# Two-input elementwise work moved from GpSimd to VectorE, and squares from GpSimd to ScalarE, in a hybrid DeltaNet trunk

## The chip, the cores and the metric

The kernel runs on one core of a Trainium2 chip. The metric is the device time of one execution in microseconds; the median of three runs is taken. The profile gives the span of one profiled execution, from its first to its last instruction.

## The reference

One layer works on 256 tokens of width 2048, in float32. The part that the change touches is the first RMS norm and the gated DeltaNet branch:

```python
h = rms_norm(x, norm_mix_g)             # x * rsqrt(mean(x * x)) * gain
z = h @ w_in                            # 2048 -> all branches' inputs
qkv = silu(causal_depthwise_conv(gdn_qkv, conv_w))
...
decay = exp(where(incl, g[:, None] - g[None, :], -inf))
L = where(strict, (k * beta) @ k.T * decay, 0)
sol = triangular_solve(L + eye, rhs, lower=True, unit_diagonal=True)
intra = (q @ k.T) * decay
# then a scan over chunks: v_new = u - w S;  o = q_dec S + intra v_new;  S = S exp(g) + k_dec v_new
```

Eight heads of dimension 128 go through this. Beside it stand a spatial gating branch and a stick-breaking attention branch; gates, output projections and a squared-ReLU MLP of width 8192 follow. Those are not touched.

## The kernel before

Every product with a weight matrix is streamed. A block of weights is loaded on SP's queue into `raw` (three buffers), ScalarE rounds a piece of it into `hi` (line 154), VectorE takes the rest into `lo` (the subtraction in `split_w`, recorded under line 65, the helper `tt`), and TensorE multiplies with both. `hi` and `lo` have six buffers each, and a piece is split four pieces ahead of its use (`LA = 4`). So ScalarE's `hi` waits until TensorE has given a buffer back, VectorE's `lo` waits for `hi`, and TensorE's next piece waits for `lo`.

Everything else, the DeltaNet among it, is background work: generators in the queue `side`, from which `pump` takes one step after each piece of a product. On TensorE the order is the order in which the code is written, the product pieces and the background steps interleaved. On the other engines the framework's scheduler writes the order of each engine's queue ahead of time; only in the first product are VectorE's and ScalarE's own instructions kept in the order of the code too. Each engine then runs its queue strictly in order on the chip.

In the first product x arrives in eight chunks of two 128-row tiles. For each, `split_scaled` writes the high part on ScalarE (line 239) and the low part on VectorE (line 241). After each second chunk `x_squares` squares four tiles and adds them into `sq`, on GpSimd except for the last square; the sum ends in `ssx`, which `row_norms` needs for the reciprocal row norms.

`gdn_half` does four heads, and runs twice. Its two-input work on GpSimd is: `gm` (triangle mask times gate, high and low part, for two chunks), `kb`, `rkm` and the scaling of the decay `dec` (named `e` in rows) for two chunks, `kde` and `kbg`, and the substitution. For the substitution the matrix `LT` goes by DMA through a DRAM scratch `scrL` into `lb`, so that the 64 diagonal blocks of 16 x 16 lie on partitions of their own; then come 15 steps of one product `pr` and one subtraction into `tb`, 30 instructions each of which needs the one before:

```python
for j in range(15):
    n, m = 15 - j, j + 1
    pv = pr[:, 0 : n * m].rearrange("p (i s) -> p i s", i=n)
    tt(pv, lb[:, j, m:16].unsqueeze(2)..., tb[:, j : j + 1, 0:m]..., ALU.mult, nc.gpsimd)
    tt(tb[:, m:16, 0:m], tb[:, m:16, 0:m], pv, ALU.subtract, nc.gpsimd)
    if j % 2:
        yield
```

`tb` and its transpose `ub` (a GpSimd copy) go back through `scrT` and `scrU` into `Tm` and `Um`, by DMAs on GpSimd's queue. TensorE's first product with `Tm` stands at a fixed place in TensorE's order, after a number of product pieces. `add_halves` and `conv_silu` share three buffers (`half`) that ScalarE fills and VectorE empties.

Of the kernel before, what the change touches and what calls it, by code (L numbers as in the profile page):

```python
# [15 lines left out]
P = 128  # L16
# [4 lines left out]
def tile_hybrid_trunk(  # L21
# [47 lines left out]

    # ------------------------------------------------ background work queue  # L70
    side = deque()
# [9 lines left out]
    def pump_until(n):  # L81
        """run until at most n pieces of background work are left"""
        while len(side) > n:
            pump(1)
# [7 lines left out]

    # ------------------------------------------------ constants
    ident = cp.tile([P, P], F32, name="ident")
# [5 lines left out]

    # the tensor engine is clocked up only under work: give it some while the first loads run
    ones = cp.tile([P, P], F32, name="ones")
# [15 lines left out]
    def split_T(dst, k0, nk, pt, scale=None):  # L118
        """dst[:, k0:k0+nk] = the exact high and low parts of the (scaled) psum tile pt [P, nk, 256]"""
        if scale is None:  # L120
            nc.scalar.copy(dst[:, k0 : k0 + nk, 0, :], pt)
            tt(dst[:, k0 : k0 + nk, 1, :], pt, dst[:, k0 : k0 + nk, 0, :].bitcast(F32), ALU.subtract)
        else:
            for i in range(nk):
                s = scale[:, k0 + i : k0 + i + 1]
                nc.scalar.activation(dst[:, k0 + i, 0, :], pt[:, i, :], AF.Copy, scale=s)
            for i in range(nk):
                s = scale[:, k0 + i : k0 + i + 1]
                nc.vector.scalar_tensor_tensor(
                    dst[:, k0 + i, 1, :], pt[:, i, :], s, dst[:, k0 + i, 0, :].bitcast(F32),  # L130
                    op0=ALU.mult, op1=ALU.subtract,
                )

    # ------------------------------------------------ streamed products
    # Weights are split into exact high and low parts LA pieces ahead of the products that use them.
    LA = 4
# [7 lines left out]
    def flush():  # L144
        while pipe:
            pipe.popleft()()
# [11 lines left out]
    def gemm(lhs, w, b, done, before=None, rate=0):  # L158
        """done([psum of token tile t]) gets act times block b of w, tokens on partitions"""
        ps = []  # L160
# [32 lines left out]
    def gemm_T(act, w, b, done, g0=0, ng=None, rate=0):  # L193
        """done([psum of 128 columns each]) gets (act times block b of w)^T, its low-part half on the right"""
        ps = []
# [38 lines left out]

    # ------------------------------------------------ x^T and its row norms
    def split_scaled(dst, src, scale, k0, nk):
        """dst[:, k] = the exact high and low parts of scale[:, k] src[:, k]"""
        for k in range(k0, k0 + nk):
# [16 lines left out]
    def x_chunk(c, stage):  # L255
# [4 lines left out]
        else:  # L260
            split_scaled(actT, xs, g1, 2 * c, 2)
            if c % 2:
                x_squares(c // 2)

    hl = lhs_of(actT)
# [11 lines left out]
    def row_norms():  # L277
        """1 / rms of x's rows, along the free axis (rb) and on partitions (r1); then they scale the first product"""
        yield from rest(10)
# [12 lines left out]
        yield  # L292

    def x_squares(c):
        s4 = xp.tile([P, 4, T], F32, tag="sqc", name="sqc", bufs=2) if c else sq
        xc = xs[:, 4 * c : 4 * c + 4]
        if c < 3:
            tt(s4, xc, xc, ALU.mult, nc.gpsimd)
        else:
            nc.scalar.activation(s4, xc, AF.Square)  # L300
        if c:
            tt(sq, sq, s4, ALU.add, nc.gpsimd)
        if c == 3:
            tt(sq[:, 0:2], sq[:, 0:2], sq[:, 2:4], ALU.add, nc.gpsimd)
            tt(ssx, sq[:, 0], sq[:, 1], ALU.add, nc.gpsimd)

# [7 lines left out]
    with tc.manual_schedule(engines={ET.PE, ET.DVE, ET.Activation}):  # L314
        gemm(hl, w_ag0, 0, first_done, before=x_chunk, rate=1)
    flush()
    xctx.close()
    nc.gpsimd.dma_start(ab_bc, a_dt.partition_broadcast(P).rearrange("p o h -> p (o h)"))

    # ------------------------------------------------ more constants  # L320
    tri_gt_full = cp.tile([P, P], F32, name="tri_gt_full")
# [17 lines left out]

    # ------------------------------------------------ branch inputs, transposed  # L340
    brctx = ExitStack()
    brp = brctx.enter_context(tc.tile_pool(name="brp", bufs=1))
    aT = brp.tile([P, 8, 2, T], F32R, name="aT")

    # ================================================ gated DeltaNet
    gt0ctx = ExitStack()
# [3 lines left out]

    # lvl[b][s, c] = 1 where s lies in the first and c in the second half of one 2b block, in 64 x 64 blocks
    lvl = {}
# [24 lines left out]

    # scratch for moving the 16 x 16 diagonal blocks of a 64 x 64 block onto partitions of their own and back
    NB = 64
# [26 lines left out]
    def gates_ab():  # L406
# [9 lines left out]
        nc.scalar.activation(nega, ab_bc[:, 0:8], AF.Exp)  # L416
        # log1p(e) = 2 artanh(e / (2 + e))
        d = gp.tile(sh, F32, name="sp_d")
# [31 lines left out]
    def conv_silu(zt, cb0, dst):  # L450
        """causal convolution along the free axis, and SiLU; zt [P, 4, T] is scaled by the row norms first"""
        for j in range(4):
# [17 lines left out]
    def gdn_half(hf, tiles):  # L470
        """heads 4 hf .. 4 hf + 3, in chunks of 128, as tiles come in"""
        hs = slice(4 * hf, 4 * hf + 4)
# [23 lines left out]

        # decay[s, c] = exp(g_c - g_s) for s <= c
        dec = []
        ck = conv_silu(tiles["k"], 8 + 4 * hf, kTt)
        for t in range(NT):  # L500
            gms = []
            for part in (gh.bitcast(F32), gl):
                gm = t2k("gm", F32R)
                tt(gm, col(tri_le), row(part[:, t, hs]), ALU.mult, nc.gpsimd)
                gms.append(gm)
# [29 lines left out]
        for t in range(NT):  # L535
            kb = t2k("kb")
            tt(kb, kraw[:, t], row(brk[:, t]), ALU.mult, nc.gpsimd)
            rkm = t2k("rkm")
            tt(rkm, col(tri_le), row(rk[:, t]), ALU.mult, nc.gpsimd)
            tt(dec[t], dec[t], rkm, ALU.mult, nc.gpsimd)  # L540
            kbs.append(kb)
            yield
# [24 lines left out]

        # T = (I + L)^-1 and U = T^T: 16 x 16 blocks by substitution, then doubled to 128
        lb = gp.tile([NB, 16, 16], F32, tag="lb", name="lb")
# [21 lines left out]
        for j in range(15):  # L591
# [5 lines left out]
                tb[:, j : j + 1, 0:m].broadcast_to([NB, n, m]),  # L597
                ALU.mult, nc.gpsimd,
            )
            tt(tb[:, m:16, 0:m], tb[:, m:16, 0:m], pv, ALU.subtract, nc.gpsimd)  # L600
            if j % 2:
# [14 lines left out]
        kde = gp.tile([P, 4, HD], F32, tag="kde", name="kde")  # L616
        tt(kde, kraw[:, 0], row(f2), ALU.mult, nc.gpsimd)
        tt(kbg, kraw[:, 1], row(f1), ALU.mult, nc.gpsimd)
        tiles["k free"] = True
# [25 lines left out]
        for b in (16, 32):  # L645
# [4 lines left out]
            yield from rest(2)  # L650
            # the last level takes T's first block only
            parts, ps_ = ((0, 1), slice(0, P)) if b == 16 else ((0,), slice(0, 64))
# [22 lines left out]

        # u = T (beta v); w^T = (beta e^g k)^T T^T for the second chunk
        u = gp.tile(H4, F32, tag="u", name="u")
# [12 lines left out]
        tiles["v free"] = True  # L690
        # the state after the first chunk, and what the second takes from it
        S = gp.tile([P, 4, HD], F32, tag="M", name="S")
# [14 lines left out]
        yield from rest(2)  # L707
        # output: o = e^g q S + intra v_new, normalized and gated
        o = gp.tile(H4, F32, tag="o", name="o")
# [41 lines left out]
    def scaled_T(pt, dst):  # L751
        """dst = pt's sum of halves times the rows' 1 / rms"""
        add_halves(dst, pt)
        tt(dst, dst, rb, ALU.mult)
# [18 lines left out]
    def heads_T(c0, key, tiles, rate, last=None, ready=None):  # L773
        """columns c0 .. c0 + 512 of q, k and v, transposed, into tiles[key]"""
        zt = [None]
# [39 lines left out]

    # ================================================ spatial gating
    RU = 1
# [87 lines left out]

    # ================================================ stick-breaking attention
    sctx = ExitStack()
# [126 lines left out]

    # ================================================ branch gates and the branches' products
    for br in range(3):
# [48 lines left out]

    # ================================================ output projection, residual
    fin = {}
# [17 lines left out]
    def second_norm():  # L1105
        """r2 = 1 / mean square of the rows: relu(r z)^2 = r^2 relu(z)^2 for the row factor r > 0"""
        yield from rest(5)
# [36 lines left out]

    # ================================================ squared-ReLU MLP
    NQ = 4
# [40 lines left out]
def _laid_out(inputs):  # L1187
# [4 lines left out]
    def by_partition(v):  # L1192
        """[128 k, ...] as [128, k, ...]"""
        return v.reshape(v.shape[0] // P, P, *v.shape[1:]).swapaxes(0, 1)

    def tiles(w, kg, width):
        """[K, C] as [C / width, K / (128 kg), 128, kg, width]"""
        k, c = w.shape
# [52 lines left out]
```

## Time and profile before

| what | value |
|---|---|
| median of 3 runs | 1724.08 us (1722.41 to 1724.3) |
| span of the profiled execution | 1722.3 us; no time of its own is given beside it, the lowest run is 0.1 us above it |
| PE busy | 1697.8 us (99%) |
| DVE busy | 1186.4 us (69%) |
| ACT busy | 963.9 us (56%) |
| POOL busy | 169.5 us (10%), 225 instructions |
| mean granted TensorE clock | 0.994 |

PE is TensorE, DVE is VectorE, ACT is ScalarE, POOL is GpSimd. The DeltaNet ends some 360 us into the span; the first product of x ends at 28 us.

### The profile page before, as it was taken

What the parts mean: (1) busy time and instruction counts of PE and PEld (TensorE: products, weight loads), DVE (VectorE), ACT (ScalarE), POOL (GpSimd) and SP (SyncE); (2) the same over time, 40 slices, a digit from 0 to 9 for tenths busy, and PEclk for the clock granted to TensorE, in tenths of its full rate; (3) what the DMA queues carried; (4) which work ended last, traced back from release to release, by engine and by line L of the source; (5) the groups of instructions that cost most, each with busy time, mean ns of one, the idle gap of its engine ahead of it and who ended that gap; (6) DMA issues with size and microseconds to landing.
All of it is one profiled execution on the core that took longest, in us unless ns stands there. A gap on an engine that the chain in (4) does not pass through costs nothing.

```text
span 1722.3 us, 26815 instructions
## 1 busy us (share of the span) xinstructions
PE 1697.8 (99%) x9880; PEld 1480.8 (86%) x9880; DVE 1186.4 (69%) x2174; ACT 963.9 (56%) x1741; POOL 169.5 (10%) x225
## 2 busy tenths in 40 slices
PE   8998999999999999999999999999999999999999
PEld 7887888888888888888888888888888888888887
DVE  8885688466658666666787777666776677567764
ACT  5774576465567665555555555544554455445543
POOL 7134024000001000001222100000000000000000
PEclk9999999999999999999999999999999999999999
DMA  7445355355444455555556555555555555555563
GB/s 244 180 144 166 107 179 190 114 189 193 173 170 172 154 189 178 189 191 177 179 209 226 194 196 186 185 192 196 187 186 190 196 192 182 191 194 191 183 217 119
DMA packets 48211, 313.77 MB, mean 182 GB/s; under 512 B 5600, under 2 KB 7792, under 8 KB 12240
## 3 DMA queue, kind: packets, MB, share of 16 engines
q1 hardware_dynamic: 46224, 306.41, 51.2%
q0 software_dynamic: 1856, 5.65, 1.1%
q8 instruction: 77, 1.26, 0.3%
q14 instruction: 54, 0.44, 0.1%
HBM read 308.62 MB, written 3.42 MB: 181 GB/s over the span
## 4 chain that ended last, share of the span: by engine, by line
PE 90%; DVE 3%; DMA 3%; POOL 2%; issue 1%; ACT 1%; DVEq 0%; POOLq 0%; ACTq 0%
PE g L62 86%; PE pm L62 3%; DVE lo L65 1%; POOL tb L65 1%; POOL pr L65 1%; DMA Tm<-scrT 1%; DMA scrU<-ub 1%; DMA lb<-scrL 1%; DMA scrL<-LT 1%; ACT hi L154 0%; DVE qkT L65 0%; DMA ab_bc<-in_a_dt_dram 0%; ACT hT L239 0%; PE pm L928 0%; DVE qkT L458 0%
## 5 line engine op out<-in xcount | busy, mean ns | idle before, releaser
L65 DVE TENSOR_TENSOR lo<-raw,hi 128x512 fp32r<-128x512 f32 (+2 forms) x1168 | 815.3, 705 | 474.5 <-ACT hi L154 469.6
L154 ACT CAST hi<-raw 128x512 fp32r<-128x512 f32 (+2 forms) x1168 | 708.9, 615 | 613.6 <-PE g L62 559.6
L62 PE MATMUL g<-hT,hi 128*128 128x512 f32 x1280 | 464.1, 405 | 0.0
L62 PE MATMUL g<-hT,lo 128*128 128x256 f32 x1280 | 363.2, 284 | 6.8 <-DVE lo L65 6.8
L62 PE MATMUL g<-h2T,hi 128*128 128x512 f32 x1024 | 355.4, 394 | 0.0
L62 PE MATMUL g<-fT,hi 128*128 128x512 f32 x1024 | 355.2, 394 | 0.0
L62 PEld LDWEIGHTS g<-hT,hi 128*128 128x128 f32 x1280 | 243.8, 190 | 58.2
L62 PE MATMUL g<-h2T,lo 128*128 128x256 f32 x1024 | 284.2, 278 | 0.0
L62 PE MATMUL g<-fT,lo 128*128 128x256 f32 x1024 | 284.1, 277 | 0.0
L62 PEld LDWEIGHTS g<-hT,lo 128*128 128x128 f32 x1280 | 245.2, 192 | 9.4 <-DVE lo L65 9.1
L62 PEld LDWEIGHTS g<-fT,hi 128*128 128x128 f32 x1024 | 192.1, 188 | 44.4
L62 PEld LDWEIGHTS g<-h2T,hi 128*128 128x128 f32 x1024 | 192.1, 188 | 44.4
L62 PE MATMUL g<-hi,hT 128*128 128x512 f32 (+2 forms) x704 | 216.5, 379 | 2.8 <-ACT hT L239 1.9
L62 PEld LDWEIGHTS g<-h2T,lo 128*128 128x128 f32 x1024 | 192.4, 188 | 0.0
L62 PEld LDWEIGHTS g<-fT,lo 128*128 128x128 f32 x1024 | 192.4, 188 | 0.0
L62 PEld LDWEIGHTS g<-hi,hT 128*128 128x128 f32 x704 | 130.5, 189 | 23.4 <-ACT hT L239 2.1
L62 PE MATMUL g<-lo,hT 128*128 128x512 f32 (+2 forms) x352 | 131.6, 374 | 1.4 <-DVE lo L65 1.4
L62 PE MATMUL g<-yT,hi 128*128 128x512 f32 x256 | 88.8, 391 | 0.0
L225 ACT COPY half<-g 128x256 f32<-128x256 f32 x192 | 70.4, 369 | 22.8 <-PE g L62 14.7
L62 PEld LDWEIGHTS g<-lo,hT 128*128 128x128 f32 x352 | 66.8, 190 | 11.4 <-DVE lo L65 2.0
L62 PE MATMUL g<-yT,lo 128*128 128x256 f32 x256 | 71.8, 281 | 0.0
L65 DVE TENSOR_TENSOR x<-x,g 128x256 f32<-128x256 f32 x160 | 57.2, 415 | 9.0 <-PE g L62 6.4
(299 smaller groups left out, 1455.6 us busy)
## 6 DMA issues: line engine op xcount, KB each, us to landing
raw<-in_w_ff_dram SPq DMA_DIRECT2D x128, 1024.0 KB, 4.8
raw<-in_w_gl_dram SPq DMA_DIRECT2D x48, 1024.0 KB, 4.8
raw<-in_w_qkv_dram SPq DMA_DIRECT2D x24, 1024.0 KB, 4.9
raw<-in_w_sba_dram SPq DMA_DIRECT2D x24, 1024.0 KB, 4.8
raw<-in_w_out_dram SPq DMA_DIRECT2D x16, 1024.0 KB, 4.8
raw<-in_w_v_dram SPq DMA_DIRECT2D x8, 1024.0 KB, 4.7
raw<-in_w_u_dram SPq DMA_DIRECT2D x8, 1024.0 KB, 4.8
raw<-in_w_out_a_dram SPq DMA_DIRECT2D x8, 1024.0 KB, 4.8
```

The costliest lines, as they stand in the source:

```text
L62: nc.tensor.matmul(out, lhsT, rhs, start=start, stop=stop)
L65: (eng or nc.vector).tensor_tensor(out, a, b, op=op)
L154: nc.scalar.copy(hi, rw)
L225: nc.scalar.copy(tmp, pt[:, T : 2 * T])
```

## The change

All two-input instructions of GpSimd in the first product and in `gdn_half` go to VectorE (`tt` without an engine). The squares of x all go to ScalarE, and their additions are put off by one chunk. The last additions stand inside the stretch in which the code's order holds on VectorE and ScalarE, with the `flush` in front of them. GpSimd keeps its memsets, masks, the copy into `ub` and all its DMAs. Comments and docstrings are deleted too; they emit nothing.

```diff
@@ x_chunk
             if c % 2:
                 x_squares(c // 2)
+            elif c:
+                sum_x_squares()
@@
+    squares = deque()
+
     def x_squares(c):
         s4 = xp.tile([P, 4, T], F32, tag="sqc", name="sqc", bufs=2) if c else sq
-        xc = xs[:, 4 * c : 4 * c + 4]
-        if c < 3:
-            tt(s4, xc, xc, ALU.mult, nc.gpsimd)
-        else:
-            nc.scalar.activation(s4, xc, AF.Square)
-        if c:
-            tt(sq, sq, s4, ALU.add, nc.gpsimd)
-        if c == 3:
-            tt(sq[:, 0:2], sq[:, 0:2], sq[:, 2:4], ALU.add, nc.gpsimd)
-            tt(ssx, sq[:, 0], sq[:, 1], ALU.add, nc.gpsimd)
+        nc.scalar.activation(s4, xs[:, 4 * c : 4 * c + 4], AF.Square)
+        squares.append(s4)
+
+    def sum_x_squares():
+        s4 = squares.popleft()
+        if s4 is not sq:
+            tt(sq, sq, s4, ALU.add)
@@
     with tc.manual_schedule(engines={ET.PE, ET.DVE, ET.Activation}):
         gemm(hl, w_ag0, 0, first_done, before=x_chunk, rate=1)
-    flush()
+        flush()
+        sum_x_squares()
+        tt(sq[:, 0:2], sq[:, 0:2], sq[:, 2:4], ALU.add)
+        tt(ssx, sq[:, 0], sq[:, 1], ALU.add)
@@ gdn_half
-                tt(gm, col(tri_le), row(part[:, t, hs]), ALU.mult, nc.gpsimd)
+                tt(gm, col(tri_le), row(part[:, t, hs]), ALU.mult)
@@
-            tt(kb, kraw[:, t], row(brk[:, t]), ALU.mult, nc.gpsimd)
+            tt(kb, kraw[:, t], row(brk[:, t]), ALU.mult)
             rkm = t2k("rkm")
-            tt(rkm, col(tri_le), row(rk[:, t]), ALU.mult, nc.gpsimd)
-            tt(dec[t], dec[t], rkm, ALU.mult, nc.gpsimd)
+            tt(rkm, col(tri_le), row(rk[:, t]), ALU.mult)
+            tt(dec[t], dec[t], rkm, ALU.mult)
@@ the substitution
-                ALU.mult, nc.gpsimd,
+                ALU.mult,
             )
-            tt(tb[:, m:16, 0:m], tb[:, m:16, 0:m], pv, ALU.subtract, nc.gpsimd)
+            tt(tb[:, m:16, 0:m], tb[:, m:16, 0:m], pv, ALU.subtract)
@@
-        tt(kde, kraw[:, 0], row(f2), ALU.mult, nc.gpsimd)
-        tt(kbg, kraw[:, 1], row(f1), ALU.mult, nc.gpsimd)
+        tt(kde, kraw[:, 0], row(f2), ALU.mult)
+        tt(kbg, kraw[:, 1], row(f1), ALU.mult)
```

## Rows read from the trace of the kernel before

**Rows 1.** The page, part 1: busy time and share of the span by engine.

```profile
PE 1697.8 (99%) x9880; PEld 1480.8 (86%) x9880; DVE 1186.4 (69%) x2174; ACT 963.9 (56%) x1741; POOL 169.5 (10%) x225
```

**Rows 2.** Waits of PE, 0 to 360 us: total us, times, longest us.

```profile
PE g L62 <- DVE lo L65: 8.2, 7, 3.4
```

**Rows 3.** Waits of PE, 0 to 40 us, the same columns.

```profile
PE g L62 <- DVE lo L65: 3.1, 4, 1.4
...
PE g L62 <- DVE hT L241: 0.9, 1, 0.9
```

**Rows 4.** Timeline of PE, four places: start us, us, operation, [idle before].

```profile
101.29 0.58 PE L62 MATMUL g<-hT,lo 128*128 128x256 f32 x1 [3.43 <-DVE lo L65]
...
158.64 0.59 PE L62 MATMUL pm<-Tm,CT 64*64 64x64 f32 x6 [4.69 <-DMA Tm<-scrT]
...
251.60 0.39 PE L62 MATMUL g<-hT,lo 128*128 128x256 f32 x1 [1.20 <-DVE lo L65]
...
303.47 0.74 PE L62 MATMUL pm<-Tm,CT 64*64 64x64 f32 x18 [2.67 <-DMA Tm<-scrT]
```

**Rows 5.** Busy time by stretch: us, engines' busy us (instructions), PEclk, DMA share, GB/s.

```profile
6.00:40.00 34.00, 28.70 (x149) 24.68 (x150) 31.65 (x41) 21.92 (x50) 28.89 (x41) 0.95 0.74 265
...
100.00:108.00 8.00, 6.71 (x24) 5.81 (x25) 6.39 (x14) 5.68 (x11) 0.35 (x1) 0.57 0.27 89
127.90:142.90 15.00, 15.00 (x91) 13.32 (x90) 10.73 (x18) 10.13 (x19) 12.68 (x30) 1.00 0.71 256
158.00:168.00 10.00, 9.36 (x112) 8.21 (x113) 2.32 (x4) 1.82 (x3) 0.00 (x0) 0.66 0.23 76
303.00:309.00 6.00, 5.53 (x46) 4.72 (x46) 0.81 (x2) 1.58 (x3) 0.00 (x0) 0.72 0.40 161
```

**Rows 6.** Groups on DVE by form, 6 to 40 us: busy us, mean ns, idle before.

```profile
L65 DVE TENSOR_TENSOR lo<-raw,hi 128x352 fp32r<-128x352 f32 x16 | 12.6, 822 | 5.5 <-ACT hi L154 5.5
L65 DVE TENSOR_TENSOR lo<-raw,hi 128x512 fp32r<-128x512 f32 x9 | 11.7, 1359 | 1.7 <-ACT hi L154 1.7
```

**Rows 7.** Groups on DVE by form, 89.7 to 100.5 us.

```profile
L65 DVE TENSOR_TENSOR lo<-raw,hi 128x512 fp32r<-128x512 f32 x2 | 3.2, 1624 | 0.0
L65 DVE TENSOR_TENSOR qkT<-qkT,z 128x253 f32<-128x253 f32 x3 | 2.8, 941 | 0.0
L458 DVE SCALAR_TENSOR_TENSOR qkT<-zq,vec,qkT 128x255 f32<-128x255 f32 x2 | 2.5, 1255 | 0.0
```

**Rows 8.** Groups on DVE by form, 400 to 1700 us.

```profile
L65 DVE TENSOR_TENSOR lo<-raw,hi 128x512 fp32r<-128x512 f32 x918 | 636.4, 697 | 372.1 <-ACT hi L154 367.8
...
L65 DVE TENSOR_TENSOR ff<-sT,r 128x256 f32<-128x256 f32 x64 | 27.0, 423 | 1.1
```

**Rows 9.** Groups on POOL by form, whole span.

```profile
L65 POOL TENSOR_TENSOR sq<-sq,sqc 128x1024 f32<-128x1024 f32 x3 | 7.4, 2462 | 0.1
...
L65 POOL TENSOR_TENSOR gm<-tri_le,gh 128x512 fp32r<-128x512 f32 x4 | 5.2, 1310 | 68.9 <-PE pm L62 42.7 <-DVE gh L436 26.1
```

**Rows 10.** Timeline of ACT, two places.

```profile
21.39 1.06 ACT L300 ACTIVATE sqc<-xs 128x1024 f32<-128x1024 f32 x1 [0.85 <-POOL sq L65]
...
96.97 0.37 ACT L225 COPY half<-g 128x256 f32<-128x256 f32 x1 [3.94 <-DVE qkT L65]
```

**Rows 11.** Timeline of POOL: the substitution's ends in both halves, and `sq`.

```profile
8.38 1.89 POOL L65 TENSOR_TENSOR sq<-xs 128x1024 f32<-128x1024 f32 x1 [5.91 <-DMA xs<-in_xT_dram]
...
116.33 1.47 POOL L572 DMA_DIRECT2D scrL<-LT  x2 [15.98 <-DVE LT L65]
...
127.94 0.21 POOL L65 TENSOR_TENSOR pr<-lb,tb 64x15 f32<-64x15 f32 x1 [3.33 <-DMA lb<-scrL]
...
142.34 0.55 POOL L65 TENSOR_TENSOR tb<-tb,pr 64x15 f32<-64x15 f32 x1
```

**Rows 12.** Timeline of DVE: small instructions that need each other.

```profile
55.69 0.17 DVE L419 TENSOR_SCALAR sp_d<-sp_e 128x16 f32<-128x16 f32 x1 [0.83 <-ACT sp_e L414]
55.89 0.25 DVE L421 RECIPROCAL sp_rd<-sp_d 128x16 f32<-128x16 f32 x1
```

## The prediction

> **What bounds the kernel now.** I read the busy times first: TensorE is busy 99% of the span, so any gain lies in the 24 us in which it is not, or in stretches where its clock is low [rows 1]. Next I read what TensorE waits for while the DeltaNet runs. Up to 360 us it waits 8.2 us in seven places for `lo`, VectorE's low part of the weights [rows 2]. In the first product that is 3.1 us, and 0.9 us more for the low part of x [rows 3]. Four other places stand in the timeline: 3.43 us for `lo` at 101 us, 1.20 us at 251 us, and 4.69 and 2.67 us for the DMA that brings `Tm`, once in each half [rows 4]. The reader should see that the first kind of wait is one for VectorE and the second one for the end of a chain that GpSimd computes.
>
> After three of these waits the clock is low. From 100 to 108 us the granted clock averages 0.57, from 158 to 168 us 0.66, and from 303 to 309 us 0.72; a clock of 1 is the level of 2.4 GHz, and the mean lies between that and half of it, 1.2 GHz [rows 5]. Taken on TensorE's busy time in these stretches, that is 6.71 x 0.43 = 2.9 us, 9.36 x 0.34 = 3.2 us and 5.53 x 0.28 = 1.5 us of work done late, beside the waits themselves.
>
> Why is VectorE late? The same subtraction of 128 x 512 into `lo` takes 697 ns where GpSimd is nearly idle [rows 8], 1359 ns from 6 to 40 us [rows 6] and 1624 ns from 89.7 to 100.5 us [rows 7]. Both slow stretches are those in which GpSimd runs two-input work on 128 partitions. VectorE is not computing more there, it is held up.
>
> **First product (gain 4.0 us).** Removed are six large GpSimd instructions of up to 2.46 us [rows 9]. The excess they cause on VectorE is 9 x (1359 - 697) ns = 6.0 us on the 128 x 512 form alone, and 16 x (822 - 500) ns = 5.2 us on the 128 x 352 form, where 500 ns is my interpolation between 423 ns for 256 columns and 697 ns for 512 [rows 6, 8]. Added on VectorE are three additions of 128 x 1024, one of 128 x 512 and one of 128 x 256. By the step of 274 ns for 256 columns, 1024 columns take 1.25 us, so the sum is 3 x 1.25 + 0.70 + 0.42 = 4.9 us [rows 8], and half of it comes after the last `lo` of this product. VectorE thus wins some 6 us. ScalarE gets three more squares of 1.06 us, in front of later `hi` [rows 10]; from 6 to 40 us it is busy for 21.92 of 34 us [rows 5], and no table load stands in front of the square that it does already, so I cost this at nothing. If that cover is gone the price is at most the 3.2 us of the squares. TensorE's waits for VectorE here are 3.1 + 0.9 = 4.0 us [rows 3], and I take them all; the bounds are 1 us (squares in the way) and 4 us.
>
> **Decay and keys (gain 1.5 + 0.5 us).** Of the eight GpSimd instructions between 89.8 and 100.4 us, two are `kb`, two `rkm`, two `dec`, and one each `kde` and `kbg`. The forms of VectorE's in that stretch lose 2 x (1624 - 697) + 3 x (941 - 423) + 2 x (1255 - 423) ns = 5.1 us [rows 7, 8]. Eight instructions of 0.70 us on VectorE cost 5.6 us, or some 4.9 us since neighbours overlap by nearly 0.1 us. So VectorE's load stays about the same, and what changes is the order: six of the eight come before the convolution of q in the code. ScalarE stood 3.94 us at the shared `half` buffer until VectorE got to that convolution [rows 10], `hi` stood behind it, then `lo`, then TensorE for 3.43 us [rows 4]. With the moved instructions ahead in VectorE's own queue this wait shrinks but doesn't vanish. Bounds: nothing won, or all of 3.43 us and the 2.9 us of clock; I take 1.5 us, nearer to nothing since the load is equal. In the second half the same eight stand before a wait of 1.20 us [rows 4]; bounds 1 us lost and 1.2 us won, I take 0.5 us. `gm`, eight instructions of 1.3 us on GpSimd [rows 9], falls where TensorE does not wait; 0.7 us each on VectorE replaces about as much hold-up, and I cost it at nothing.
>
> The Trainium skill, SBUF — State Buffer, "Summary: rules for kernel authors", says that while a GpSimd instruction reads SBUF, a VectorE instruction with two SBUF inputs fully blocks until it has finished. The rows agree in kind, but 5.1 us of hold-up stands against eight instructions that would be some 10 us by 1.3 us each [rows 7, 9], so about half. By the rule the move would free 10 - 4.9 = 5 us of VectorE here, and the wait and its slow clock would go altogether; by the rows it frees almost nothing.
>
> **The substitution (gain 9.8 us, less 4 us of a new wait).** On GpSimd the 30 dependent instructions take from 127.94 to 142.9 us, 15.0 us [rows 11]. On VectorE a small instruction that needs the one before starts 0.20 us after it [rows 12], so 30 take 6 us if nothing comes between. But VectorE is busy for 10.73 of these 15 us with its other work [rows 5]; if all of that keeps its place, 6 us of chain spread over the 28% left take 21 us. `lo` runs ahead of TensorE and can give way, and other work in the gaps hides part of the 0.20 us; I take 11 us, between 6 and 21. Then `Tm` comes 4 us earlier in each half. Of 4.69 us the first half keeps 0.7 us and, I estimate, half its slow clock: 4.0 + 1.6 = 5.6 us won. The second half loses its 2.67 us and its slow clock of 1.5 us: 4.2 us won. Together 9.8 us; the bounds are 4.69 + 2.67 + 3.2 + 1.5 = 12.1 us won, and 12 us lost at a chain of 21 us.
>
> Behind the wait for `Tm` stand TensorE's own products and the pieces of weights, so no other engine is late next.
>
> The new wait: the first `pr` now stands in VectorE's queue and waits for the DMA into `lb`. From the issue into `scrL` to the first `pr` 11.6 us pass [rows 11]. Behind it in the queue stand the next `lo`, and TensorE waits for those. The order is written ahead of time, and it trusts transfers to be quicker than they are: GpSimd's queue had the first square of x at its head when x was still 5.91 us away, and stood [rows 11]. If VectorE gets to `pr` early, it stands for several us; six `hi`/`lo` buffers cover some of it. Bounds: nothing, or 5 us in each half with the clock; I take 2 us each, 4 us.
>
> The Trainium skill, DMA: Bandwidth & Descriptors, gives about 2.0 us fixed for one DMA from GpSimd's queue. By that the two hops would take 4 us as an estimate, the data would lie ready, and the new wait would be nothing; 11.6 us in the rows speak against it.
>
> **Sum.** 4.0 + 1.5 + 0.5 + 9.8 - 4.0 = 11.8 us won. The profiled span is 1722.3 us, so 1710.5 us; the median of the runs shown is 1.8 us above that span, and so the forecast is 1712.3 us. A difference under 0.2% (3.4 us) is what a measurement of this kernel can't tell from none.
>
> **The rivals.**
> First, fuller relief: the hold-up on VectorE is all that makes the decay stage late. Then the second term is 3.43 + 2.9 = 6.3 us in place of 1.5 us: 1707.5 us, and with no new wait 1703.5 us. For it speaks that every late `lo` lies beside GpSimd work [rows 6, 7]; against it the equal load. It is what the SBUF rule above would give.
> Second, the new wait eats the substitution's gain: VectorE stands 5 us in each half, and TensorE with it. Then 10 us go against 9.8 us, and 6 us are left: 1718.3 us. For it speaks how early the queue put the square of x [rows 11].
> Third, the other side: the chain paced by `lo`. Each `lo` waits for a buffer that TensorE gives back, and chain instructions placed behind it wait too. If they get only the gaps, 21 us in place of 15 us, `Tm` is 6 us later in each half: 12 us lost against 6 us won elsewhere, 1730 us. It decides against the change from a chain of 18 us on (2 x 3 us = 6 us). For it speaks VectorE's load of 72% there [rows 5]; against it that the chain's own work is only 6 us.
> Fourth, no change: VectorE's work costs what its hold-up did, squares delay `hi`, the chain takes 14 us. Then some 2 us are won: about 1722 us.
>
> **Chances.** Forecast, within 1704 to 1717 us: 0.53. Fuller relief below 1707.5 us by its own cause: 0.10. New wait, 1717 to 1720.6 us: 0.16. No change: 0.11. Chain paced by `lo`: 0.10. So faster 0.79, same 0.11, slower 0.10. A range from 1704 to 1722 us leaves out the best end of the fuller relief, part of no change and the slower rival, about 2 in 10.
>
> **What the next profile would show.** Right: `lo` of 128 x 512 near 0.70 us everywhere up to 300 us; no wait of TensorE for VectorE before 40 us; first `pr` to last `tb` in 8 to 13 us; the wait for `Tm` under 1.5 us in the first half and gone in the second; granted clock near 1 from 300 to 310 us. Wrong: a long idle stretch of VectorE released by the DMA into `lb`, with TensorE idle behind it; a chain of over 15 us; a wait for `lo` at 95 to 105 us as long as now; ScalarE's `hi` late in the first product.

## The result, and the profile after

The changed kernel takes 1702.2 us (median of four runs, 1702.13 to 1702.36), the kernel before beside it 1723.81 us. The ratio is 0.9881, with an interval from 0.9867 to 0.9895: 21.6 us faster, where the forecast was 11.8 us. The direction was right; the gain is nearly twice the forecast, and the time lies below the range that was given.

The page, part 1, of the changed kernel (profiled span 1700.6 us); it answers to [rows 1]:

```profile
PE 1689.6 (99%) x9880; PEld 1472.7 (87%) x9880; DVE 1182.3 (70%) x2263; ACT 967.3 (57%) x1744; POOL 96.8 (6%) x133
```

VectorE got 89 instructions more and is busy 4.1 us less. TensorE executes the same 9880 products and is busy 8.2 us less, as its mean granted clock rose from 0.994 to 1.000; the rest of the gain is waits. The waits of TensorE up to 360 us, beside [rows 2] (us, times, longest):

```profile
PE g L62 <- DVE lo L65: 2.5, 7, 0.6
PE pm L62 <- DMA Tm<-scrT: 1.3, 1, 1.3
```

Of the four long waits of [rows 4] one is left, at 1.27 us. TensorE's timeline, with three milestones: the product with `ssx`, the last product of the convolved q and k of the first half (`pm<-qkT`), the first product with `Um`. The line at 93.46 us answers to the 3.43 us of [rows 4]; the one at 87.03 us had 0.42 us before.

```profile
40.83 0.59 PE L62 MATMUL pm<-ssx,ones 128*128 128x256 f32 x2
...
87.03 0.39 PE L62 MATMUL g<-hT,lo 128*128 128x256 f32 x1 [0.35 <-DVE lo L65]
...
93.46 0.39 PE L62 MATMUL g<-hT,lo 128*128 128x256 f32 x1 [0.60 <-DVE lo L65]
...
103.71 1.03 PE L62 MATMUL pm<-qkT 128*128 128x256 f32 x4
...
146.11 1.14 PE L62 MATMUL pm<-Tm,CT 64*64 64x64 f32 x30 [1.27 <-DMA Tm<-scrT]
...
150.16 1.15 PE L62 MATMUL pm<-M,Um 64*64 64x64 f32 x32
```

In the kernel before the same three stand at 46.24, 113.81 and 165.54 us. So 5.4 us are won by the first, 10.1 by the second, 15.4 by the third, 17.3 by the end of q and k in the second half (243.83 against 261.09 us), and the rest, some 4.4 us, behind that. The windows, as in [rows 5], show a clock of 1.00 at the places that were slow:

```profile
6.00:40.00 34.00, 31.95 (x179) 27.96 (x180) 28.87 (x54) 26.54 (x57) 9.28 (x24) 1.00 0.87 321
86.00:94.00 8.00, 7.04 (x39) 5.35 (x38) 8.00 (x19) 6.23 (x14) 0.00 (x0) 1.00 0.27 89
94.00:102.00 8.00, 7.95 (x45) 6.85 (x44) 8.00 (x19) 5.60 (x10) 0.00 (x0) 1.00 0.50 166
145.00:155.00 10.00, 8.89 (x126) 7.81 (x126) 4.10 (x7) 2.57 (x5) 0.00 (x0) 1.00 0.61 208
283.00:289.00 6.00, 6.00 (x108) 5.17 (x108) 3.30 (x7) 3.09 (x6) 0.00 (x0) 1.00 0.62 220
```

VectorE's instructions by form from 80 to 100 us, which hold the stretch of [rows 7]:

```profile
L65 DVE TENSOR_TENSOR lo<-raw,hi 128x512 fp32r<-128x512 f32 x9 | 6.2, 686 | 0.2 <-ACT hi L154 0.2
...
L65 DVE TENSOR_TENSOR qkT<-qkT,z 128x253 f32<-128x253 f32 x4 | 1.7, 416 | 0.0
...
L65 DVE TENSOR_TENSOR kb<-kraw,brk 128x512 f32<-128x512 f32 x2 | 1.4, 687 | 0.0
```

The same subtraction that took 1624 ns takes 686 ns, and a moved instruction takes 687 ns where GpSimd took some 1.3 us. The chain of the substitution on VectorE, its first two instructions and its last:

```profile
117.13 0.17 DVE L65 TENSOR_TENSOR pr<-lb,tb 64x15 f32<-64x15 f32 x1 [3.22 <-DMA lb<-scrL]
...
117.62 0.17 DVE L65 TENSOR_TENSOR tb<-tb,pr 64x15 f32<-64x15 f32 x1
...
132.38 0.16 DVE L65 TENSOR_TENSOR tb<-tb,pr 64x15 f32<-64x15 f32 x1
```

The feared wait for `lb` is there, 3.22 us (1.52 us in the second half), but behind it TensorE stands only 0.19 us. And the chain takes 15.4 us, as long as on GpSimd [rows 11]; in the second half 13.3 us, against 14.9 us on GpSimd.

### The profile page after: what moved, and what is told of

Its sections match the earlier page's. It is cut to its first block, busy times and chain, and to the rows that moved or that the text cites. A ratio compares the mean times of both kernels' runs of the same rounds, so it can differ in the third digit from the quotient of the medians.

```text
span 1700.6 us, 26821 instructions
## 1 busy us (share of the span) xinstructions
PE 1689.6 (99%) x9880; PEld 1472.7 (87%) x9880; DVE 1182.3 (70%) x2263; ACT 967.3 (57%) x1744; POOL 96.8 (6%) x133
## 3 DMA queue, kind: packets, MB, share of 16 engines
HBM read 308.62 MB, written 3.42 MB: 183 GB/s over the span
## 4 chain that ended last, share of the span: by engine, by line
PE 93%; DVE 3%; DMA 2%; ACT 1%; issue 1%; POOL 0%; SPq 0%; DVEq 0%; POOLq 0%; ACTq 0%
PE g L62 89%; PE pm L62 3%; DVE lo L65 1%; ACT hi L154 0%; DMA Tm<-scrT 0%; DMA scrT<-tb 0%; DMA xs<-in_xT_dram 0%; DMA lb<-scrL 0%; DMA scrL<-LT 0%; ACT hT L239 0%; PE pm L933 0%; DVE qkT L463 0%; DVE Z L65 0%; DVE tb L65 0%; DVE vT L463 0%
## 5 line engine op out<-in xcount | busy, mean ns | idle before, releaser
L65 DVE TENSOR_TENSOR lo<-raw,hi 128x512 fp32r<-128x512 f32 (+2 forms) x1168 | 796.7, 689 | 450.6 <-ACT hi L154 444.1
L62 PE MATMUL g<-hT,hi 128*128 128x512 f32 x1280 | 458.0, 401 | 0.0
L62 PE MATMUL g<-hT,lo 128*128 128x256 f32 x1280 | 359.6, 281 | 1.1 <-DVE lo L65 1.1
L62 PEld LDWEIGHTS g<-hT,lo 128*128 128x128 f32 x1280 | 241.7, 189 | 3.2 <-DVE lo L65 2.9
```

Of the source, the lines that this page charges most:

```text
L62: nc.tensor.matmul(out, lhsT, rhs, start=start, stop=stop)
L65: (eng or nc.vector).tensor_tensor(out, a, b, op=op)
```

## The experiments

In brackets stands the ratio to the kernel before, run beside on the same chip, with its interval. A difference to the changed kernel is taken to the 1702.2 us of its own measurement; as the medians of the kernel before, beside the runs, lie between 1722.9 and 1723.8 us, such a difference of under 1 us says nothing.

### Each part by itself

Three kernels are the kernel before with one part of the change's diff each.

**x_only**: the squares of x and their additions (first three hunks).

```diff
-            tt(s4, xc, xc, ALU.mult, nc.gpsimd)
+        nc.scalar.activation(s4, xs[:, 4 * c : 4 * c + 4], AF.Square)
...
-            tt(sq, sq, s4, ALU.add, nc.gpsimd)
+            tt(sq, sq, s4, ALU.add)
```

> Only the squares of x and their sums are moved. The forecast's first term gives 4.0 us won, about 1719.8 us, with no wait of VectorE's in the first product. The profile of the changed kernel shows 5.4 us won by the row norms' product, which also holds a start at the full clock: if that belongs to the change, 1718.4 us; if the start is chance, 1720 to 1721 us.

Measured: 1717.92 us (0.9971 [0.9957, 0.9984]), 5.5 us won. The product with `ssx` starts at 40.86 us, as in the changed kernel; the wait for `lo` is still 3.43 us (at 95.98 us) and `Tm` is still waited for, 7.6 us in all. Before 40 us TensorE still waits 1.1 us for `lo`. The first term has the right cause and is 1.5 us too small.

**keys_only**: `gm`, `kb`, `rkm`, `dec`, `kde` and `kbg` on VectorE.

```diff
-            tt(kb, kraw[:, t], row(brk[:, t]), ALU.mult, nc.gpsimd)
+            tt(kb, kraw[:, t], row(brk[:, t]), ALU.mult)
...
-            tt(dec[t], dec[t], rkm, ALU.mult, nc.gpsimd)
+            tt(dec[t], dec[t], rkm, ALU.mult)
```

> Only gm, kb, rkm, dec, kde and kbg are moved. Theory of the forecast (equal load, later by order): 2.0 us won, 1721.8 us. Theory of the hold-up (VectorE waits on GpSimd's reads, the wait for lo at 101 us and its slow clock are all of that cause): 6 to 8 us won, 1716 to 1718 us, and no wait for lo over 1 us between 85 and 110 us; the wait for Tm stays or shrinks only by what LT comes earlier.

Measured: 1712.73 us (0.9941 [0.9926, 0.9955]), 10.7 us won, where the forecast had 2.0 us. TensorE's timeline at the places of [rows 4]:

```profile
94.00 0.39 PE L62 MATMUL g<-hT,lo 128*128 128x256 f32 x1 [0.34 <-DVE lo L65]
...
100.43 0.38 PE L62 MATMUL g<-hT,lo 128*128 128x256 f32 x1 [0.60 <-DVE lo L65]
...
154.35 1.96 PE L62 MATMUL pm<-Tm,CT 64*64 64x64 f32 x30 [3.56 <-DMA Tm<-scrT]
```

The wait of 3.43 us for `lo` is down to 0.60 us (at 100.43 us), the one of 1.20 us is gone, and the wait for `Tm` in the first half is 1.1 us shorter. In the second half the wait for `Tm` is gone too, although the substitution is still on GpSimd: `LT` goes out at 256.63 us for a first product with `Tm` at 293.94 us, 1.6 us more room than before (264.80 and 300.47 us), and from there to the issue of the second half of `Tm` it takes 2.1 us less. Between the two traces TensorE wins 4.7 us around the first wait for `lo`, 1.5 us around the first wait for `Tm`, 1.9 us around the second for `lo` and 4.5 us around the second for `Tm`, and has lost 1.6 us at the start (the `ssx` product at 47.83 us): 11.0 us between the spans, 1722.3 and 1711.3 us.

**chain_only**: the 30 instructions of the substitution on VectorE.

```diff
-                ALU.mult, nc.gpsimd,
+                ALU.mult,
...
-            tt(tb[:, m:16, 0:m], tb[:, m:16, 0:m], pv, ALU.subtract, nc.gpsimd)
+            tt(tb[:, m:16, 0:m], tb[:, m:16, 0:m], pv, ALU.subtract)
```

> Only the substitution is moved. Forecast's theory (the chain gets 4 us shorter, a new wait for the data takes part of it back): 5.8 us won, 1718 us, a chain of 11 us. Rival (the chain is no shorter on VectorE, 15.4 and 13.3 us in the changed kernel): within 1.5 us of before, 1722 to 1725 us, and the wait for Tm is there as before.

Measured: 1715.04 us (0.9956 [0.9944, 0.9968]), 8.3 us won. `Tm` is waited for only 0.9 us in all. Here the new wait does show, 2.08 us at 129 us, where `lo` was queued behind the wait for `lb`:

```profile
101.39 0.39 PE L62 MATMUL g<-hT,lo 128*128 128x256 f32 x1 [3.42 <-DVE lo L65]
...
129.04 0.43 PE L62 MATMUL g<-lo,hT 128*128 128x344 f32 x1 [2.08 <-DVE lo L65]
```

In chain_only the chain itself did get shorter in the first half, 12.9 us against 15.0 us. The three alone add up to 24.5 us, 2.9 us more than together; keys and chain both take away the second half's wait for `Tm`, and that counts once. The excess itself is not clear of noise, as the interval of each is some 2 us to either side.

### Each part put back

**x_back**: the changed kernel with the squares of x on GpSimd as before (x_only's diff reversed).

> The changed kernel with the first product's squares, their additions and x times rx back on GpSimd as before; the keys and the substitution stay moved. If the x part is worth what it was worth alone (5.5 us): 1707 to 1708 us, and the product with ssx again at about 46 us in place of 40.8. By the forecast's first term (4.0 us): 1706 us. The rival, that the x part's gain was a chance of the clock at the kernel's start: within 1.5 us of the changed kernel (1701 to 1704 us).

Measured: 1707.84 us (0.9911 [0.9897, 0.9926]), 5.6 us over the changed kernel; the `ssx` product starts at 46.39 us. The part is worth the same from both sides.

**chain_back**: the changed kernel with the substitution on GpSimd (chain_only's diff reversed).

> The changed kernel with the substitution back on GpSimd. Forecast's theory: 5.8 us lost, 1708 us, and the waits for Tm are back at 4.7 and 2.7 us. Rival (the chain's engine matters little, Tm came in time since LT did): 1702 to 1704 us, waits for Tm of 0 to 2 us.

Measured: 1706.82 us (0.9905 [0.9891, 0.992]), 4.6 us over the changed kernel. GpSimd's timeline:

```profile
133.80 0.87 POOL L608 DMA_DIRECT2D scrT<-tb  x1 [0.29 <-POOL tb L65]
...
136.91 0.68 POOL L616 DMA_DIRECT2D Tm<-scrT  x1
141.58 0.68 POOL L617 DMA_DIRECT2D Um<-scrU  x1 [3.99 <-DMA scrU<-ub]
142.26 0.68 POOL L616 DMA_DIRECT2D Tm<-scrT  x1
```

`tb` is finished here less than a microsecond later than in the changed kernel (issue into `scrT` at 133.80 against 133.06 us). The chain takes 15.4 us on either engine. What is late is the second transfer into `Tm`: the code issues `Tm`, `Um`, `Tm`, `Um`, and the first `Um` holds the queue 3.99 us until `scrU` has landed. TensorE waits 3.95 us for `Tm`, and the clock behind it is low in two windows:

```profile
146.00:150.00 4.00, 1.89 (x30) 1.78 (x30) 0.00 (x0) 0.00 (x0) 0.00 (x0) 0.53 0.29 47
150.00:156.00 6.00, 6.00 (x73) 5.22 (x74) 1.69 (x3) 1.83 (x3) 0.00 (x0) 0.75 0.14 25
```

The wait is 3.95 - 1.27 = 2.7 us longer, and the clock costs 1.89 x 0.47 + 6.00 x 0.25 = 2.4 us; together 5.1 us for 4.6 us measured. So in this place it is the queue and the clock that pay, and not the length of the chain.

### Reads or time: what holds VectorE up

**dummy_reads**: the changed kernel with eight added GpSimd products of 128 x 512 in each half, where the keys stood, into a tile that nobody reads.

```diff
+        dm = gp.tile([P, 4, HD], F32, tag="LT", name="dm")
+        for i in range(8):
+            tt(dm, kraw[:, i % 2], row(brk[:, i % 2]), ALU.mult, nc.gpsimd)
```

> The changed kernel, and in each half GpSimd does eight products of 128x512 with two inputs in SBUF, at the place where kb, rkm, dec, kde and kbg stood, into a tile that nobody reads. Theory of the hold-up (VectorE stands while GpSimd reads): VectorE's load grows by 5 us in each half, the wait for lo near 90 us is 3 us or more again with a low clock behind it, 6 to 12 us lost, 1708 to 1714 us. Rival (GpSimd's results were late, and that made VectorE and TensorE late): nothing depends on these, so 1702 to 1703 us.

**dummy_writes**: the same place, eight memsets, which read nothing (the small copy on VectorE, 0.16 us, only holds them in their place).

```diff
+        dm = gp.tile([P, 1024], F32, tag="LT", name="dm")
+        nc.vector.tensor_copy(dm[:, 0:4], f2)
+        for i in range(8):
+            nc.gpsimd.memset(dm, 0.0)
```

> The same place, but eight memsets of 128x1024 on GpSimd: as long on the engine, with no input. Theory of the hold-up by reads: VectorE isn't held, 1702 to 1703 us, lo at 0.69 us. Rival (any work of GpSimd's holds VectorE up): like the run with two inputs, 1708 us or more.

Measured: reads 1714.76 us (0.9962 [0.995, 0.9973]), 12.6 us over the changed kernel; writes 1702.55 us (0.9887 [0.9872, 0.9902]), within 0.4 us of it. VectorE's forms from 80 to 100 us, first with the reads, then with the writes:

```profile
L65 DVE TENSOR_TENSOR lo<-raw,hi 128x512 fp32r<-128x512 f32 x6 | 5.8, 961 | 0.2 <-ACT hi L154 0.2
...
L65 DVE TENSOR_TENSOR rkm<-tri_le,rn 128x512 f32<-128x512 f32 x2 | 3.1, 1526 | 0.0
```

```profile
L65 DVE TENSOR_TENSOR lo<-raw,hi 128x512 fp32r<-128x512 f32 x10 | 6.8, 680 | 0.2 <-ACT hi L154 0.2
...
L65 DVE TENSOR_TENSOR rkm<-tri_le,rn 128x512 f32<-128x512 f32 x2 | 1.4, 681 | 0.0
```

And the longest wait that returns with the reads, against 0.60 us in the changed kernel:

```profile
92.03 0.58 PE L62 MATMUL g<-hT,lo 128*128 128x256 f32 x1 [4.11 <-DVE lo L65]
```

VectorE's timeline with the reads shows what a hold-up is, two of seven instructions in a row:

```profile
84.67 1.52 DVE L65 TENSOR_TENSOR lo<-raw,hi 128x512 fp32r<-128x512 f32 x1
86.12 1.52 DVE L65 TENSOR_TENSOR e<-e,rkm 128x512 f32<-128x512 f32 x1
```

They start 1.45 us apart, and that is the time of one GpSimd product (11.64 / 8): the two engines take turns, one instruction each. The memsets keep GpSimd busy 8.06 us in each half and cost nothing; the products keep it busy 11.64 us and cost 12.6 us, more than the 10.7 us that the keys are worth, since VectorE has the moved work here as well as the hold-up. GpSimd's reads hold VectorE, not its activity. That the products take `LT`'s buffer delays nothing: they end at 94.3 us, and `LT` is first written at 106.2 us. The Trainium skill, SBUF — State Buffer, "Who interferes with whom", says that an instruction of VectorE with two SBUF inputs contends with a GpSimd instruction that reads SBUF and not with one that only writes it; both runs agree, with `rkm` at 1526 and 681 ns.

### The order of the transfers into Tm and Um

**tm_first** (the changed kernel), **chain_back_tm_first** (chain_back) and **before_tm_first** (the kernel before) each get the same edit:

```diff
         for a in range(2):
             s_ = slice(64 * a, 64 * a + 64)
             nc.gpsimd.dma_start(Tm[s_], scr_main("T", a))
+        for a in range(2):
+            s_ = slice(64 * a, 64 * a + 64)
             nc.gpsimd.dma_start(Um[s_], scr_main("U", a))
```

> The changed kernel; only the order of four DMA issues on GpSimd's queue differs: both halves of Tm before both of Um, so that Tm's second half no longer stands behind the landing of ub in scrU. The wait of 1.3 us for Tm goes: 1700.9 us if nothing else hangs on it, no gain (1702.2 us) if the landing of Tm itself ends the wait.

> The substitution on GpSimd, with the same order of DMA issues. If the 4.7 us that the move of the substitution is worth came from the tail behind it (the second half of Tm standing behind scrU's landing, and the clock after a wait of 3.9 us), this comes to 1701 to 1703 us. If it came from the substitution itself on VectorE, it stays at 1705 to 1707 us.

Measured: tm_first 1701.69 us (0.9881 [0.9866, 0.9896]), not told apart from the changed kernel, with no wait for `Tm` left. chain_back_tm_first 1700.36 us (0.9874 [0.9857, 0.989]; runs from 1700.12 to 1700.59), with no such wait either, though the substitution runs on GpSimd again. This is the fastest kernel of the study. All its waits for `lo` up to 360 us:

```profile
PE g L62 <- DVE lo L65: 1.5, 4, 0.6
```

With the transfers in the right order, moving the substitution is worth nothing; on the same chip it costs 1.3 us (tm_first's runs lie from 1701.06 to 1701.85), and the first product with `Um` stands at 149.34 us against 147.99 us without the move.

> The kernel before with one edit: both transfers into Tm are issued ahead of both into Um on GpSimd's queue. If TensorE waited for Tm only because Tm's second half stood behind the issue that waited 4.39 us for scrU to land, both waits for Tm (4.69 and 2.67 us) and the low clock behind them go: 8 to 12 us less, 1711 to 1715 us. The rival, by which the substitution and its landings are themselves too long on GpSimd: the waits stay within a microsecond and the time is within 2 us of the kernel before (1721 to 1725 us). What the wait for lo (3.43 us at 94 us) costs should stay in both cases.

Measured: 1718.11 us (0.9967 [0.9953, 0.998]), but nine executions lie in two groups: three at 1711.9 to 1712.1 us, six at 1717.7 to 1719.3 us. The trace of one at 1712.1 us shows no wait for `Tm`. Two more single executions were made to get a trace of the other group.

> The kernel before with both transfers into Tm issued ahead of both into Um, once more, since its executions lie in two groups, at 1712 and at 1718 us, and the trace that there is belongs to the lower. One theory: an execution at 1718 us shows the waits for Tm again (over 2 us each), and the order of the queue alone doesn't settle them. The rival: it shows no wait for Tm, and the 6 us lie in the wait for lo at 94 us and in a lower clock behind it (0.57 as in the kernel before in place of 0.79) and at the start.

> The same kernel for a further trace, with the same two theories: near 1718 us, either waits for Tm of over 2 us, or none and a longer wait for lo or a lower clock behind it. Near 1712 us it tells nothing new.

Measured: 1711.05 and 1718.05 us. GpSimd's timeline in the quick and in the late execution:

```profile
128.26 0.21 POOL L65 TENSOR_TENSOR pr<-lb,tb 64x15 f32<-64x15 f32 x1 [3.53 <-DMA lb<-scrL]
...
143.65 0.87 POOL L603 DMA_DIRECT2D scrT<-tb  x1 [0.34 <-POOL tb L65]
...
147.84 1.36 POOL L611 DMA_DIRECT2D Tm<-scrT  x2 [1.55 <-DMA scrT<-tb]
```

```profile
129.40 0.21 POOL L65 TENSOR_TENSOR pr<-lb,tb 64x15 f32<-64x15 f32 x1 [4.66 <-DMA lb<-scrL]
...
145.71 0.87 POOL L603 DMA_DIRECT2D scrT<-tb  x1 [0.29 <-POOL tb L65]
...
149.70 1.36 POOL L611 DMA_DIRECT2D Tm<-scrT  x2 [1.12 <-DMA scrT<-tb]
```

`lb` lands 1.1 us later, the substitution loses another 0.9 us, and then the two transfers into `Tm` take 6.7 us to land (median) in place of 3.1 us. TensorE waits 3.84 us, and the window behind it shows a clock of 0.55:

```profile
156.39 0.47 PE L62 MATMUL pm<-Tm,CT 64*64 64x64 f32 x2 [3.84 <-DMA Tm<-scrT]
```

```profile
155.00:160.00 5.00, 3.34 (x35) 2.94 (x36) 0.00 (x0) 0.59 (x1) 0.00 (x0) 0.55 0.32 53
```

In the second half of this execution TensorE waits only 0.18 us for `Tm`. So in the kernel before both theories hold in part. In its one trace the order of the queue makes the wait of the first half, and without that order the chain ends so near TensorE's place that the landing of two transfers decides. x_only has the old order and the chain on GpSimd too, and there the first `Um` does not wait for `scrU` at all; TensorE waits for the landing of the first half of `Tm`, issued at 144.63 us:

```profile
150.43 0.33 PE L62 MATMUL pm<-Tm,CT 64*64 64x64 f32 x2 [3.15 <-DMA Tm<-scrT]
```

In the second half of the kernel before the `Um` issue holds the queue only 0.75 us, of a wait of 2.67 us.

## Why the prediction was right in direction and wrong in size

**What bounds.** Right in the main: but for some of the first product's 5.4 us, the gain lies in the four long waits of [rows 4], the clock behind them [rows 5], and the small waits of [rows 3]. The bounds of the terms add to 4.0 + 6.3 + 1.2 + 12.1 = 23.6 us, and 21.6 us were won.

**First product.** Right in mechanism: 5.5 us by itself, 5.6 us when put back, for 4.0 us. The step "I take them all" did not hold: before 40 us the changed kernel still waits 1.4 us for `lo`, so 2.6 of the 4.0 us went. That the sum came out near is in part luck; the other 2.9 us were not traced to a row. The squares of 1.04 us on ScalarE are hidden, no table load stands in front of them, and VectorE's additions take 1.23, 0.70 and 0.43 us, as estimated. The clock of this stretch is no explanation: it was 0.95 before [rows 5] and is 1.00 after, but the `ssx` product stands at 40.8 to 41.2 us in every traced version with this part and at 46.2 us or later in every one without, also where the start ran at a low clock.

**Decay and keys: the step that failed.** "So VectorE's load stays about the same" led to "nearer to nothing since the load is equal", 2.0 us; by itself this part won 10.7 us. The first half of the step was right: from the last `f` to the end of the convolution of q VectorE takes 13.9 us in the kernel before (89.69 to 103.56 us) and 13.1 us in keys_only (89.56 to 102.70 us), and is busy throughout in both. What does not follow is that nothing is won. Before, the hold-up falls on `lo` and the convolution just when `half` and `hi` hang on them, and VectorE starts a `lo` at 90.16 and 93.91 us and the next only at 100.55 us. In keys_only it starts one at 90.85, 93.25, 94.85, 96.96 and 99.68 us, and gets two more done in the stretch. In the changed kernel VectorE is busy for all of the two windows from 86 to 102 us, and yet TensorE waits only 0.35 and 0.60 us there.

The order of ScalarE's queue, written ahead of time, changed as well. In the kernel before, `half` at 96.97 us [rows 10] stands in front of four pieces of `hi`, which start at 98.82 us; in the changed kernel three pieces stand in front of `half`:

```profile
87.42 1.65 ACT L154 CAST hi<-raw 128x512 fp32r<-128x512 f32 x3
89.78 0.37 ACT L225 COPY half<-g 128x256 f32<-128x256 f32 x1 [0.71 <-DVE qkT L65]
```

dummy_reads has this new order and the hold-up, and loses 12.6 us with a wait of 4.11 us: the hold-up by reads is enough, and the order alone does not protect from it. What the order adds where there is no hold-up, no run shows.

The part had a second gain that was not in the term: the second half's wait for `Tm` and its clock went as well (2.67 + 1.5 us), which the prediction had booked under the substitution. The first rival, fuller relief, named the mechanism of the first gain. Its 1703.5 us with no new wait lie within 1.3 us of the measurement by luck: 4.0, 6.8 and 9.8 us for the three parts, where 5.5, 10.7 and 8.3 us were measured by themselves and 4.6 us for the last when put back.

**The rule on SBUF.** The prediction set the rule of the Trainium skill, SBUF — State Buffer, "Summary: rules for kernel authors", against the rows, found half of the hold-up, and let the rows decide. That comparison was not sound. It left out a form in the same stretch (two instructions of 254 columns, 1.03 us in place of some 0.47), so the hold-up is some 6.2 us and not 5.1. And its 1.3 us for a GpSimd product hold waiting too: the shortest `gm` takes 1.04 us, and in dummy_reads, where the engines take turns, a product takes 1.45 us, of which 0.60 us are VectorE's own step from start to start. The hold of 1526 - 686 = 0.84 us is what is left of that turn, so these rows agree with an engine that stands until the other's instruction has ended. The rule's result in the prediction, that the wait and its clock go, is nearly what happened: 0.60 us of wait at a clock of 1.00. The error was to turn microseconds of hold-up into microseconds of the kernel; what counted was which instruction was held.

**The substitution: right sum, wrong mechanism.** 9.8 us less 4 us was forecast; put back, it is worth 4.6 us, by itself 8.3 us. But the chain did not shorten to 11 us: it takes 15.4 us, because the order written ahead put twelve `lo` of 128 x 512 and twelve other instructions between its links (VectorE is busy 15.23 us of that stretch). The gain came from GpSimd's queue: in the changed kernel `scrU` has landed by the time the first `Um` is to be issued, and `Tm`'s second transfer goes out at 140.14 us, against 142.26 us in chain_back. The prediction read the wait for `Tm` as "the end of a chain that GpSimd computes" and overlooked the order of the four issues behind it. chain_back_tm_first settles it for the changed kernel.

**The new wait.** It came, at 3.22 us of VectorE in the first half, and cost TensorE 0.19 us in place of 2 us. In chain_only, with the keys still on GpSimd, the same wait cost 2.08 us. That the six buffers cover it when VectorE is not late already fits both, but was not tested by itself. The second page that the prediction cited, the Trainium skill, DMA: Bandwidth & Descriptors, "Anatomy of one DMA — SWDGE (gpsimd) path", would have the data ready, by about 2.0 us for one DMA; the waits of 3.22 and 1.52 us speak against it here too.

**The rivals on the other side.** A chain of 18 us, the point from which the third would decide, was not reached; that nothing would change is excluded by the interval.

## What to carry to other kernels

Price a hold-up by the instruction that it delays and by what waits for that one, not by the microseconds of the engine's load: nearly the same load on VectorE, free of hold-up, was worth 10.7 us. Before a chain is moved to a faster engine, read the issues behind its end in their queue's order; here, with the keys moved, four issues in another order did as much as the move of the chain. And where a wait just disappears, take several executions: what is near its margin comes back with the landing of a transfer.

## What was not expected of the hardware

What a wait of TensorE's costs in clock could not be read from its length. The same wait for `lo`, 3.42 to 3.44 us, ends at 101.3 to 101.4 us in five traces and at 95.98 us in x_only. In the kernel before the clock behind it is 0.57 [rows 5]. In the three traces of before_tm_first it is 0.79, and in x_only and chain_only 1.00, here before_tm_first and chain_only:

```profile
100.00:108.00 8.00, 6.70 (x28) 5.78 (x29) 6.38 (x14) 5.68 (x11) 0.36 (x1) 0.79 0.27 89
100.00:108.00 8.00, 6.12 (x32) 5.14 (x33) 6.38 (x14) 5.69 (x11) 0.46 (x1) 1.00 0.27 89
```

From the end of this wait to the last product of q and k 12.5 us pass in the kernel before, 11.3 to 11.5 us in before_tm_first and 10.8 us in chain_only. So the clock cost some 1.8 us here, where the prediction's way of counting gives 2.9 us, and in some executions it cost nothing. Behind shorter waits the clock was as low: 0.72 behind 2.67 us [rows 5] and 0.72 behind 1.99 us (dummy_reads, 238 to 244 us); behind 1.27 us, in the changed kernel, it was 1.00.

The landing of the same transfers through GpSimd's queue took from 3.1 to 6.7 us (two of 128 KB into `Tm`, median) while the weights streamed. In before_tm_first the late execution that was traced had lost 1.9 us before these issues, and the landing added 3.6 us. Two quick executions and one late one were traced, so that this is what splits the two groups is likely, and not shown.

Why the kernel before varies by up to 9 us from run to run (1717.79 to 1726.46 us), while the four runs of the changed kernel lie within 0.3 us, was not tested. The traces offer two sources, the clock behind the wait for `lo` and the landing of transfers that TensorE waits for.
